# Choosing between GpSimd and VectorE by the port that they share, in a hybrid attention and state-space layer

## The chip, the cores and the metric

The kernel runs on 1 core of one Trainium2 chip. The metric is the device time of one execution in microseconds (us), lower is better. A core has TensorE (PE in the profile, its weight loads PEld), VectorE (DVE), ScalarE (ACT), GpSimd (POOL) and SyncE (SP), which issues the DMAs.

## The reference

One layer over 1024 tokens of width 2048, in float32. The input is projected once, and the columns are split into an attention group and a state-space group.

```python
u = jnp.einsum('bsd,de->bse', h, w_in[layer])
q, k, v, z_attn, q_idx, k_idx, w_idx, z_ssd, xbc, dt_raw = _split_cols(u, IN_WIDTHS)
# rotary positions on a quarter of each head of q, k, q_idx and k_idx
logits = jax.nn.relu(jnp.einsum('bqhd,bsd->bqhs', qib, k_idx32))        # 16 indexer heads
score = jnp.einsum('bqhs,bqh->bqs', logits, wb)                          # then the top 256 keys
...
o_attn = _dsa_attention(q, k, v, q_idx, k_idx, w_idx) * jax.nn.silu(z_attn)
# depthwise conv, chunked scan, gate, grouped RMS norm
o_ssd = _ssd_mixer(xbc, z_ssd, dt_raw, conv_w[layer], conv_b[layer], dt_bias[layer], ...)
mixed = jnp.concatenate([o_attn, o_ssd], axis=-1)
sub = jnp.einsum('bse,ed->bsd', mixed, w_out[layer])
h = _layer_norm(DEEPNORM_ALPHA * h + sub, ln_g[layer], ln_b[layer])
```

## The kernel before, in words

The tokens are worked in two halves of 512 (`h` is 0 or 1). Each float32 operand of a projection is split into a rounded part and a residue, `hi` and `lo`, and three matmuls stand for one product: hi times hi, hi times lo, lo times hi. ScalarE makes `hi` by a copy (`fl.act`); `lo` is `raw - hi`, an operation with two operands in SBUF. The tiles are called `wr` (raw weights), `wh` and `wl` (their two parts), `xh` and `xl` (the input's or the mixed groups' parts), `pj` (projection in PSUM), `a` and `o` (other PSUM tiles, three and one), `u` and `s4` (working tiles in SBUF, of 512 and 1024 columns; the profile writes `s4` as `s`), `cv` (conv input) and `sm` (small columns).

TensorE's stream is the projections (`emit_t`, 128 columns of the weights at a time, two pieces of 1024 columns of `wr` each), later the output projection (`emit_o`). Into it the kernel weaves tasks: rotary positions and indexer scores (`t_misc`, `t_qi`, `t_score`), the selection of keys (`t_topk`), attention (`t_kv`, `t_attn`), the state-space groups (`t_xbc`, `t_ssd`) and the layer norm.

No engine's order is written out by hand. While the program is built, `Flow` keeps a clock for each engine (`Sim`), with a price for each operation, and emits a task's next step when its inputs are done by those clocks and its engines are not too far ahead. So a price or a choice of engine changes the order of all engines after it. On the chip each engine runs its own list in order and waits for semaphores.

`Sim` also models a port to SBUF that VectorE and GpSimd share: `Port.take` moves an operation behind the one that holds the port, and `shares_port` says which operations need it. On GpSimd it is every one with an SBUF operand, on VectorE one with two SBUF operands, or a `tensor_scalar` or copy from SBUF to SBUF. `pick` chooses between the two engines for the residues `wl` and `xl`. All other operations have an engine written into the code: the rotary product with the sine table, one half of the indexer queries' residue, the residues of keys, values and queries, the second of two decay products (`"VG"[k]`), and the sums and gates of the state-space groups go to GpSimd. Every instruction is recorded by one helper, so that the profile gives L290 for all; the tiles tell them apart.

Of the kernel before, what the change touches and what calls it, by code (L numbers as in the profile page):

```python
# [13 lines left out]
ALU = mybir.AluOpType  # L14
# [3 lines left out]
HALF = 512  # L18
P = 128
# [11 lines left out]
N4 = 9  # L31
WAHEAD = 2
KEEP = (0, 0)
WBIAS = 0.0


SKEW = 6
# [63 lines left out]
def in_psum(x):  # L101
    return "PSUM" in str(x.space)
# [10 lines left out]
class Sim:  # L113
# [107 lines left out]
    def shares_port(self, eng, op, outs, ins, n):  # L221
        sb = [x for x in ins if not in_psum(x) and x.free_size() > 1]
        if eng == "G":
            return op != "memset" and len(sb) > 0
        if n < 16 or op in ("max", "match_replace"):
            return False
        if op in ("tensor_scalar", "tensor_copy"):
            return n > 128 and len(sb) == 1 and not in_psum(outs[0])
        return len(sb) >= 2

    def run(self, eng, op, outs, ins, kw):
# [99 lines left out]
class Flow:  # L331
# [92 lines left out]
    def signal(self, e):  # L424
        self.signals.append(e)

    def pick(self, n, bias=0.0):


        if any(e[2] == "V" and e[0] > max(self.t, e[3] + 200) for e in self.sim.port.busy):  # L430
            return "V"
        g = max(self.clk["G"], self.t) + 180 + 2.16 * n
        v = max(self.clk["V"], self.t) + 145 + 1.042 * n
        return "G" if g + bias < v else "V"

    def pump(self, room=2000.0):
        end = self.t + room
# [74 lines left out]
def f32(ap):  # L512
    return ap.bitcast(F)


class Layer:
# [76 lines left out]
    def w_split(self, i):  # L593
        fl = self.fl
        kind, h, t, u = self.stream[i]
        raw = self.wraw.pop(i)
        hi = fl.new("wh" if fl.slots["wh"] else "s4", [P, 1024], R)
        if self.kept(i):
            fl.act(hi, raw)
            fl.free(raw)  # L600
            self.w[i] = hi, self.wlo.pop(i)
            return
        lo = fl.new("wl" if fl.slots["wl"] else "s4", [P, 1024], R)
        cols = [slice(c * 256, (c + 1) * 256) for c in range(4)] if i == 0 else [slice(0, 1024)]
        for c in cols:
            fl.act(hi[:, c], raw[:, c])
            self.sub(fl.pick(c.stop - c.start, WBIAS), lo[:, c], raw[:, c], f32(hi[:, c]))
        cell = fl.last
        fl.free(raw)
        if h == 0 and self.keep(kind, t):  # L610
            fl.add(self.t_keep(kind, t, u, lo, Event(cell)), 1, "keep")
        self.w[i] = (hi, lo)
# [35 lines left out]
    def x_split(self, k):  # L648
        fl = self.fl
        if self.xh[k] is not None:  # L650
            fl.free(self.xh[k], self.xl[k])
            fl.settle(fl.t)
        hi, lo = fl.new("xh", [P, HALF], R), fl.new("xl", [P, HALF], R)
        raw = self.raws.pop(k)
        fl.act(hi, raw)
        self.sub(fl.pick(HALF), lo, raw, f32(hi))
        fl.free(raw)
        self.xh[k], self.xl[k] = hi, lo

# [256 lines left out]
    def rope(self, x, ps, tmp, cos, sin, perm):  # L916

        fl = self.fl
        self.nc.vector.stream_shuffle(tmp, ps, perm)
        yield Need("VG")  # L920
        fl.tt("V", ps, ps, cos, ALU.mult)
        fl.tt("G", tmp, tmp, sin, ALU.mult)
        yield Need("V")
        fl.tt("V", x, ps, tmp, ALU.add)

# [88 lines left out]
    def t_qi(self, h, j, ps):  # L1014
        fl = self.fl
        n = 256 if h == 0 else 512
        s0 = 512 - n
        yield Need("A", u=4, keep=3)
        cos, sin = self.table("ri", h)
        x, tmp = fl.new("u", [P, n]), fl.new("u", [P, n])  # L1020
        a1, a2 = fl.new("u", [P, n], R), fl.new("u", [P, n], R)
        yield Need("V")
        yield from self.rope(x, ps[:, 0:n], tmp, cos[:, s0:], sin[:, s0:], self.SW8)
        fl.free(ps)
        yield Need("A")
        fl.act(a1[0:64], x[0:64])
        fl.act(a2[64:128], x[64:128])
        yield Need("VG")
        self.sub("V", a1[64:128], x[0:64], f32(a1[0:64]))
        self.sub("G", a2[0:64], x[64:128], f32(a2[64:128]))  # L1030
        fl.free(x, tmp)
        blocks = (2, 3) if h == 0 else (4, 5, 6, 7)
        if h not in self.score:
            yield Need("", **({"u": 2} if h == 0 else {"s4": 4}))
            if h not in self.score:
                self.score[h] = {i: fl.new("u" if h == 0 else "s4", [P, 512 if h == 0 else 1024]) for i in blocks}
        if j == 7:
            fl.free(*self.tab["ri", h])
        first = True
        for hh, st in ((0, a1), (1, a2)):  # L1040
            head = 2 * j + hh
            for bi, i in enumerate(blocks):
                q0 = i * P - h * HALF - s0
                lhs = st[:, q0:q0 + P]
                for kh in range(h + 1):
                    m = min((i + 1) * P - kh * HALF, HALF)
                    yield Need("PA", a=1, ev=(self.ev_k[h], self.ev_k[0], self.ev_w[h]))
                    khh, k1, k2 = self.kk[kh]
                    b = fl.new("a", [P, 512])
                    fl.mm(b[:, 0:m], lhs, khh[:, 0:m], stop=False)  # L1050
                    fl.mm(b[:, 0:m], lhs, (k1, k2)[hh][:, 0:m], start=False)
                    fl.add(self.t_score(h, i, kh, m, head, b), 2, f"score{h}", fl.t)
        fl.free(a1, a2)
# [176 lines left out]
    def t_kv(self, h, g, st, total):  # L1230
        fl = self.fl
        w = 512 * (h + 1)
        if g == 1:
            yield Need(ev=(self.ev_att(h, 0),))
        evs = tuple(self.ev_kv[hh, g, x] for hh in range(h + 1) for x in "kv") + tuple(self.ev_q[h, 4 * g + r] for r in range(4)) \
            + tuple(self.ev_z[h, 4 * g + r] for r in range(4)) + (self.ev_mask[4 * h], self.ev_mask[4 * h + 1])
        yield Need(ev=evs, u=4 * (h + 1) + 2, keep=4)
        out = {(x, hh): [fl.new("u", [P, HALF], R) for _ in range(2)] for x in "kv" for hh in range(h + 1)}
        st["kv"] = out
        for (x, hh), (hi, lo) in out.items():  # L1240
            yield Need(u=1)
            raw = fl.new("u", [P, HALF])
            fl.dma(raw, (self.k_sc if x == "k" else self.v_sc)[hh][g])
            yield Need("A")
            fl.act(hi, raw)
            yield Need("G")
            self.sub("G", lo, raw, f32(hi))
            fl.free(raw)
        fl.signal(st["ev"])
        yield Need(ev=(self.ev_att(h, g),))  # L1250
        fl.free(*[t for pair in out.values() for t in pair])
# [5 lines left out]
    def t_attn(self, h, g, st, todo):  # L1257
        fl, nc = self.fl, self.nc
        while todo:
            i, pr = todo.pop(0)  # L1260
            n = (i + 1) * P
# [5 lines left out]
            raw, gate = rg[:, 0], rg[:, 1]  # L1267
            qq = fl.new("u", [P, 2, 2, P], R)
            qh, ql = qq[:, 0], qq[:, 1]
# [8 lines left out]
            yield Need("A")  # L1278
            fl.act(qh, raw)
            yield Need("G")  # L1280
            self.sub("G", ql, raw, f32(qh))
            yield Need("", sm=1)
            sm = fl.new("sm", [P, 16])
            scored = []
            for r in range(2):
                for half in range(-(-n // 512)):
# [3 lines left out]
                    b = fl.new("a", [P, 512])  # L1290
# [4 lines left out]
                    e = Event()  # L1295
# [20 lines left out]
            while kb < nk or ahead:  # L1316
                if kb < nk and len(ahead) < 3:
                    yield Need("P", a=1, u=1, now=True)
                    b = fl.new("a", [P, 256])
# [3 lines left out]
                    e = Event()  # L1323
# [4 lines left out]
                k0, pq, e = ahead.pop(0)  # L1328
# [13 lines left out]
            for r in range(2):  # L1342
                e = 4 * g + heads[r]
# [68 lines left out]
    def t_ssd(self, h, g):  # L1412
        fl, nc = self.fl, self.nc
        sd = getattr(self, f"sd{h}")
        parts = [self.conv[h, g, j] for j in range(4)] + [self.zg[h, g, j] for j in range(2)]
        xs, bt, ct = [parts[0][0], parts[1][0]], parts[2][0], parts[3][0]
        zg = [parts[4][0], parts[5][0]]
# [9 lines left out]
        for cp in range(2):  # L1427
            cs = (2 * cp, 2 * cp + 1)
            yield Need("P", s4=1, u=5, a=1)
            ar = fl.new("s4", [P, 2, 4, P])  # L1430
            bn, xdt, xdd, hs = [fl.new("u", [P, 2, 256]) for _ in range(4)]
            ea = fl.new("u", [P, 2, 2, P])
# [6 lines left out]
            for k, c in enumerate(cs):  # L1439
                if k:  # L1440
                    yield Need("P", a=1)
                b = fl.new("a", [P, 512])
# [10 lines left out]
            b = fl.new("a", [P, 256])  # L1453
# [4 lines left out]
            cbm = bn[:, :, 128:256]  # L1458
# [7 lines left out]
            for k, c in enumerate(cs):  # L1466
# [4 lines left out]
                b = fl.new("a", [P, 256])  # L1471
# [16 lines left out]
            fl.act(ea, ea, AF.Exp)  # L1488
            yield Need("VG")
            for k, c in enumerate(cs):  # L1490
                fl.tt("VG"[k], ar[:, k], ar[:, k], cbm[:, k][:, None, :].to_broadcast([P, 4, P]), ALU.mult)
            k0 = 0 if hcur[0] is not None else 1
            yield Need("P", o=1, a=1)
            b = fl.new("a", [P, 2, 2, P])
# [19 lines left out]
            cl = slice((2 * cp + k0) * P, (2 * cp + 2) * P)  # L1514
            for j in range(2):
                y3 = xs[j][:, cl].rearrange("p (k l) -> p k l", l=P)
                fl.tt("G", y3, y3, ea[:, k0:, j], ALU.add)
            fl.free(bn, xdt, xdd, ea)
            if cp == 0:
                hs0 = hs  # L1520
# [2 lines left out]
        fl.free(hs0, hs)  # L1523
        yield Need("G")
        for j in range(2):
            fl.tt("G", xs[j], xs[j], zg[j], ALU.mult)
        yield Need("A")
        for j in range(2):
            fl.act(zg[j], xs[j], AF.Square)
        yield Need("G")  # L1530
        fl.tt("G", zg[0], zg[0], zg[1], ALU.add)
        yield Need("P", a=1, sm=1)
        sm = fl.new("sm", [P, 4])
        b = fl.new("a", [P, 512])
# [9 lines left out]
        b = fl.new("a", [P, 512])  # L1544
# [7 lines left out]
        for j in range(2):  # L1552
            e = 8 + 2 * g + j
# [159 lines left out]
```

## Time and profile before

| | |
|---|---|
| median of 3 runs | 1815.16 us (1812.81 to 1815.38) |
| profiled execution | 1813.86 us, span 1812.0 us |
| TensorE busy | 1768.7 us, 98% |
| VectorE | 1032.4 us, 57%, 1934 instructions |
| ScalarE | 915.2 us, 51%, 1571 instructions |
| GpSimd | 464.3 us, 26%, 415 instructions |
| mean granted clock of TensorE | 0.994 |

A row of a group gives count, busy time, mean ns of one, and the idle time of its engine before it with what ended it. A row of the timeline gives start, duration, engine, operation, tiles, and in brackets an idle time and its releaser. With TensorE busy 98% of the span, the profile is read by its idle stretches: where they are, and which engine ended them.

### The profile page before, as it was taken

Reading aid. Unit: us, or ns where it says so; the run is one execution under the profiler, and the core shown is the slowest. Engines: PE = TensorE matmul, PEld = TensorE weight load, DVE = VectorE, ACT = ScalarE, POOL = GpSimd, SP = SyncE. Lnnn points to the kernel's source line nnn. Section 1 sums busy time; section 2 is a strip of 40 time slices with the busy share of each in tenths; the row PEclk is TensorE's granted clock in tenths of the full one; section 3 lists DMA queues with packets and bytes.
Section 4 is the critical chain, followed back from the end, with each engine's and each line's share of the span. In section 5 each row is a group of like instructions: output and inputs, shape, how many; then the busy total and the mean of one; then the engine's idle time right before and its main releaser. Section 6 shows DMA issues by size and latency. Waiting matters only on the chain. (4 is left out here: it accounts for less than half of the span.)

```text
span 1812.0 us, 24251 instructions
## 1 busy us (share of the span) xinstructions
PE 1768.7 (98%) x8709; PEld 1474.0 (81%) x8709; DVE 1032.4 (57%) x1934; ACT 915.2 (51%) x1571; POOL 464.3 (26%) x415
## 2 busy tenths in 40 slices
PE   9999999999999999999999999999999999999996
PEld 7878888888888878878887888778888888888885
DVE  7855565555325567766755473465546445547435
ACT  6557673433234555566577768773365333431221
POOL 5310231121213133421212132022322122332123
PEclk9999999999999999999999999999999999999998
DMA  8323334333344542222333333333344344558642
GB/s 275 115 82 105 109 111 126 111 128 120 134 146 131 192 137 76 76 67 70 99 105 109 119 111 122 117 122 140 120 155 156 110 144 131 158 173 278 222 163 93
DMA packets 120424, 238.11 MB, mean 131 GB/s; under 512 B 12784, under 2 KB 50928, under 8 KB 120304
## 3 DMA queue, kind: packets, MB, share of 16 engines
q1 hardware_dynamic: 120304, 236.57, 40.2%
q8 instruction: 68, 1.11, 0.2%
q14 instruction: 52, 0.43, 0.1%
HBM read 204.47 MB, written 32.05 MB: 131 GB/s over the span
## 5 line engine op out<-in xcount | busy, mean ns | idle before, releaser
L290 PE MATMUL pj<-xh,wh 128*128 128x512 f32 (+1 forms) x1696 | 665.0, 392 | 1.8 <-ACT xh L290 1.8
L290 PE MATMUL pj<-xh,wl 128*128 128x512 f32 (+1 forms) x1696 | 650.4, 383 | 0.6 <-DVE wl L290 0.6
L290 PE MATMUL pj<-xl,wh 128*128 128x512 f32 (+1 forms) x1696 | 650.0, 383 | 1.0 <-DVE xl L290 0.5
L290 DVE TENSOR_TENSOR wl<-wr,wh 128x1024 fp32r<-128x1024 f32 (+1 forms) x214 | 270.8, 1265 | 504.9 <-ACT wh L290 478.1
L290 ACT ACTIVATE wh<-wr 128x1024 fp32r<-128x1024 f32 (+1 forms) x272 | 283.8, 1045 | 272.9 <-PE pj L290 218.9
L290 PEld LDWEIGHTS pj<-xh,wl 128*128 128x128 f32 x1696 | 320.3, 189 | 64.8 <-DVE wl L290 1.2
L290 PEld LDWEIGHTS pj<-xh,wh 128*128 128x128 f32 x1696 | 320.7, 189 | 62.0 <-issue 2.9
L290 PEld LDWEIGHTS pj<-xl,wh 128*128 128x128 f32 x1696 | 320.9, 189 | 58.4 <-DVE xl L290 0.9
L290 POOL TENSOR_TENSOR u<-u,u 128x512 f32<-128x512 f32 (+8 forms) x164 | 177.1, 1092 | 509.5 <-DVE u L290 317.5
L290 POOL TENSOR_TENSOR wl<-wr,wh 128x1024 fp32r<-128x1024 f32 (+1 forms) x58 | 139.7, 2408 | 370.6 <-ACT wh L290 359.4
L290 PE MATMUL a<-u,u 128*128 128x512 f32 (+3 forms) x840 | 181.2, 342 | 8.9 <-DVE u L290 5.3
L290 PE MATMUL pj<-wh,xh 128*128 128x512 f32 x464 | 183.1, 395 | 0.7 <-ACT u L290 0.7
L290 PE MATMUL pj<-wl,xh 128*128 128x512 f32 x464 | 180.9, 390 | 0.0
L290 PE MATMUL pj<-wh,xl 128*128 128x512 f32 x464 | 180.8, 390 | 0.0
L290 PEld LDWEIGHTS a<-u,u 128*128 128x128 f32 x840 | 137.4, 189 | 40.9 <-DVE u L290 8.4
L290 ACT ACTIVATE u<-s,sm 128x640 bf16<-128x640 int16 (+7 forms) x132 | 130.1, 985 | 32.4 <-DVE sm L290 29.3
L290 ACT ACTIVATE u<-a 128x256 fp32r<-128x256 f32 (+3 forms) x182 | 61.7, 367 | 153.6 <-PE a L290 98.0
L290 ACT ACTIVATE u<-pj 128x512 f32<-128x512 f32 x90 | 53.4, 594 | 146.8 <-PE pj L290 127.4
L290 ACT ACTIVATE a<-a 128x512 f32<-128x512 f32 (+3 forms) x160 | 75.6, 505 | 80.5 <-PE a L290 76.2
L290 PEld LDWEIGHTS pj<-wh,xl 128*128 128x128 f32 x464 | 87.1, 188 | 18.6
L290 PEld LDWEIGHTS pj<-wh,xh 128*128 128x128 f32 x464 | 87.2, 188 | 17.6 <-ACT u L290 1.2
L290 PEld LDWEIGHTS pj<-wl,xh 128*128 128x128 f32 x464 | 87.3, 188 | 16.3
(120 smaller groups left out, 1758.2 us busy)
## 6 DMA issues: line engine op xcount, KB each, us to landing
wr<-wt SPq DMA_DIRECT2D x211, 512.0 KB, 3.3
wr<-wo SPq DMA_DIRECT2D x61, 512.0 KB, 3.7
s<-arow SPq DMA_DIRECT2D x32, 256.0 KB, 4.6
u<-mx SPq DMA_DIRECT2D x32, 256.0 KB, 4.9
u<-xn SPq DMA_DIRECT2D x32, 256.0 KB, 5.6
out<-u SPq DMA_DIRECT2D x32, 256.0 KB, 2.9
u<-arow SPq DMA_DIRECT2D x64, 64.0 KB, 4.3
mx<-u SPq DMA_DIRECT2D x16, 256.0 KB, 2.4
```

The costliest lines, as they stand in the source:

```text
L290: f(*args, **kw)
```

## The change

Four things. `shares_port` counts VectorE's operations of under 16 columns, and those of exactly 128 columns in the one-operand case. `pick` takes the operands instead of a bias: it starts from the time when they are written, and returns VectorE if VectorE holds the port anywhere between GpSimd's start and end by the model, otherwise whichever engine ends first. A helper `two` calls `pick` and emits the operation there. And the operations that had GpSimd written into the code go through `two`, or through `pick`.

```diff
-        if n < 16 or op in ("max", "match_replace"):
+        if op in ("max", "match_replace"):
             return False
         if op in ("tensor_scalar", "tensor_copy"):
-            return n > 128 and len(sb) == 1 and not in_psum(outs[0])
+            return n >= 128 and len(sb) == 1 and not in_psum(outs[0])
...
-    def pick(self, n, bias=0.0):
-        if any(e[2] == "V" and e[0] > max(self.t, e[3] + 200) for e in self.sim.port.busy):
+    def pick(self, n, *ins):
+        at = self.sim.written(*ins) + Sim.LAT
+        g = max(self.clk["G"], at)
+        end = g + 180 + 2.16 * n
+        if any(e[2] == "V" and e[1] > g and e[0] < end for e in self.sim.port.busy):
             return "V"
-        g = max(self.clk["G"], self.t) + 180 + 2.16 * n
-        v = max(self.clk["V"], self.t) + 145 + 1.042 * n
-        return "G" if g + bias < v else "V"
+        return "G" if end < max(self.clk["V"], at) + 145 + 1.042 * n else "V"
+
+    def two(self, out, a, b, op):
+        self.tt(self.pick(out.free_size(), a, b), out, a, b, op)
...
-            self.sub(fl.pick(c.stop - c.start, WBIAS), lo[:, c], raw[:, c], f32(hi[:, c]))
+            fl.two(lo[:, c], raw[:, c], f32(hi[:, c]), ALU.subtract)
...
-        fl.tt("G", tmp, tmp, sin, ALU.mult)
+        fl.two(tmp, tmp, sin, ALU.mult)
...
-        self.sub("G", a2[0:64], x[64:128], f32(a2[64:128]))
+        fl.two(a2[0:64], x[64:128], f32(a2[64:128]), ALU.subtract)
...
-            self.sub("G", lo, raw, f32(hi))
+            fl.two(lo, raw, f32(hi), ALU.subtract)
...
-                fl.tt("VG"[k], ar[:, k], ar[:, k], cbm[:, k][:, None, :].to_broadcast([P, 4, P]), ALU.mult)
+                fl.tt(fl.pick(512, ar, bn), ar[:, k], ar[:, k], cbm[:, k][:, None, :].to_broadcast([P, 4, P]), ALU.mult)
...
-                fl.tt("G", y3, y3, ea[:, k0:, j], ALU.add)
+                fl.two(y3, y3, ea[:, k0:, j], ALU.add)
...
-            fl.tt("G", xs[j], xs[j], zg[j], ALU.mult)
+            fl.two(xs[j], xs[j], zg[j], ALU.mult)
```

The query residue of `t_attn`, `x_split` and the sum of the squared gates change in the same way. In the two programs GpSimd's list shrinks from 420 instructions to 220, and VectorE's grows from 1898 to 2098; TensorE has 8406 and SyncE 777 in both.

Two places of the program, in the order of the built kernels. The first is GpSimd's list in the first indexer heads, around 50 to 75 us of the profile before; `u_62` is the sine table, `wl` a weight residue of 1024 columns. Before:

```order
L290 MEMSET u_110_726 64x512
L290 TENSOR_TENSOR u_127_809<-u_124_806,u_127_809 64x256
L290 TENSOR_TENSOR u_135_891<-u_135_891,u_62_396 128x256
L290 TENSOR_TENSOR wl_147_949<-wr_140_901,wh_146_948 128x1024
L290 TENSOR_TENSOR u_137_893<-u_134_890,u_137_893 64x256
L290 TENSOR_TENSOR u_152_993<-u_152_993,u_62_396 128x256
L290 TENSOR_TENSOR wl_162_1043<-wr_148_962,wh_161_1042 128x1024
```

VectorE's list of the changed kernel at the same weight residue, with the indexer scores (`u_101` gathers them from the PSUM tiles `a`):

```order
L289 STREAM_SHUFFLE u_139_908<-pj_130_826 128x256
L289 TENSOR_TENSOR pj_130_826<-pj_130_826,u_61_395 128x256
L289 TENSOR_TENSOR u_139_908<-u_139_908,u_62_396 128x256
L289 TENSOR_TENSOR u_138_907<-pj_130_826,u_139_908 128x256
L289 TENSOR_TENSOR wl_143_916<-wr_131_833,wh_142_915 128x1024
L289 TENSOR_SCALAR u_101_678<-a_132_854,wsc0_187 128x384
L289 SCALAR_TENSOR_TENSOR u_101_678<-a_133_857,wsc0_187,u_101_678 128x384
L289 TENSOR_TENSOR wl_147_949<-wr_137_886,wh_146_948 128x1024
L289 TENSOR_TENSOR u_140_909<-u_138_907,u_140_909 64x256
```

The residue `wl_147`, the sine products and the half of the query residue now stand in VectorE's list, between the reads that free the PSUM tiles.

The second place is the rotary position of a query head of the second half, around 1138 us of the profile before, on VectorE. Before, the product with the sine table stands in GpSimd's list, and VectorE goes on with the states (`cdec`) meanwhile:

```order
L290 STREAM_SHUFFLE u_1540_9798<-pj_1532_9706 32x512
L290 TENSOR_TENSOR pj_1532_9706<-pj_1532_9706,u_1526_9686 32x512
L290 TENSOR_TENSOR u_1519_9624<-u_1511_9593,cdec1_196 128x256
L290 TENSOR_TENSOR u_1519_9624<-u_1519_9624,a_1541_9800 128x256
L290 TENSOR_TENSOR u_1539_9797<-pj_1532_9706,u_1540_9798 32x512
```

After:

```order
L289 STREAM_SHUFFLE u_1542_9827<-pj_1534_9753 32x512
L289 TENSOR_TENSOR pj_1534_9753<-pj_1534_9753,u_1527_9726 32x512
L289 TENSOR_TENSOR u_1542_9827<-u_1542_9827,u_1528_9727 32x512
L289 TENSOR_TENSOR u_1541_9826<-pj_1534_9753,u_1542_9827 32x512
```

The whole rotary position is one run on VectorE, and nothing stands between its product and its sum.

More of the change, by code (lines that the diff above doesn't have):

```diff
@@ L33 @@
 KEEP = (0, 0)
-WBIAS = 0.0
 SKEW = 6
@@ L655, in x_split @@
         fl.act(hi, raw)
-        self.sub(fl.pick(HALF), lo, raw, f32(hi))
+        fl.two(lo, raw, f32(hi), ALU.subtract)
         fl.free(raw)
@@ L1246, in t_kv @@
             yield Need("G")
-            self.sub("G", lo, raw, f32(hi))
+            fl.two(lo, raw, f32(hi), ALU.subtract)
             fl.free(raw)
@@ L1280, in t_attn @@
             yield Need("G")
-            self.sub("G", ql, raw, f32(qh))
+            fl.two(ql, raw, f32(qh), ALU.subtract)
             yield Need("", sm=1)
@@ L1530, in t_ssd @@
         yield Need("G")
-        fl.tt("G", zg[0], zg[0], zg[1], ALU.add)
+        fl.two(zg[0], zg[0], zg[1], ALU.add)
         yield Need("P", a=1, sm=1)
```

## The prediction

> **What bounds the kernel now.** I read the busy times first, then windows, then the list of what TensorE waited for, then the timeline around its longest waits. Everything below is summed against the profiled execution (span 1812.0 us, time 1813.86 us); the median of the runs is 1815.16 us, 1.3 us more, and that is added at the end. About 0.2% (3.6 us) is what a measurement of this kernel can tell from no change.
>
> ```profile
> PE 1768.7 (98%) x8709; PEld 1474.0 (81%) x8709; DVE 1032.4 (57%) x1934; ACT 915.2 (51%) x1571; POOL 464.3 (26%) x415
> ```
>
> TensorE is the bound: 1768.7 of 1812.0 us, so 43.3 us are idle. The change leaves the number of its instructions as it is (8406 in the program before and after), and only idle time can be won. Windows say where it lies (columns: length, then busy PE, PEld, DVE, ACT, POOL, the granted clock, DMA share, GB/s):
>
> ```profile
> 0.00:50.00 50.00, 45.52 (x286) 39.49 (x287) 37.89 (x57) 30.58 (x59) 26.71 (x37) 0.97 0.78 259
> 50.00:100.00 50.00, 47.18 (x277) 40.69 (x277) 42.99 (x67) 29.64 (x54) 16.13 (x16) 0.97 0.31 105
> 650.00:700.00 50.00, 48.01 (x231) 39.33 (x229) 40.48 (x76) 29.24 (x57) 22.33 (x20) 1.00 0.30 92
> 1750.00:1800.00 50.00, 45.49 (x201) 37.36 (x199) 23.51 (x39) 4.92 (x6) 15.85 (x12) 1.00 0.27 92
> 1800.00:1812.00 12.00, 0.00 (x0) 0.00 (x0) 7.55 (x10) 2.22 (x3) 3.79 (x3) 0.53 0.38 131
> ```
>
> The first 50 us hold 4.5 us of idle time and the end 4.5 + 12.0 = 16.5 us. The last 835 rows of TensorE's program are the same in both, and so are the last rows of the other engines, where the layer norm ends, so the end stays. That leaves 43.3 - 4.5 - 16.5 = 22.3 us of short waits in between. The list of waits (total us, times, longest) names them:
>
> ```profile
> PE a L290 <- DVE u L290: 5.5, 7, 1.9
> PE a L290 <- POOL sm L290: 4.3, 2, 2.4
> PE a L290 <- ACT u L290: 4.0, 1, 4.0
> ...
> PE a L290 <- DVE s L290: 1.8, 4, 0.6
> ...
> PE a L290 <- DVE ddt L290: 1.2, 1, 1.2
> PE o L290 <- DVE sm L290: 1.2, 2, 0.8
> ...
> PE a L290 <- POOL u L290: 0.8, 1, 0.8
> ```
>
> The longest wait for VectorE, at 64.48 us, in the timeline:
>
> ```profile
> 63.38 2.38 POOL L290 TENSOR_TENSOR wl<-wr,wh 128x1024 fp32r<-128x1024 f32 x1 [1.65 <-ACT wh L290]
> 63.57 2.27 DVE L290 SCALAR_TENSOR_TENSOR sm<-dt,nea 128x64 f32<-128x64 f32 x1
> 65.77 0.60 DVE L290 TENSOR_SCALAR u<-a,wsc 128x384 f32<-128x384 f32 x1
> 66.43 1.96 PE L290 MATMUL a<-u,u 128*128 128x512 f32 x4 [1.95 <-DVE u L290]
> ```
>
> GpSimd subtracts a weight tile with two SBUF operands. VectorE's 64-column operation, which also has two, starts behind it and ends when GpSimd does, 2.27 us later; the evacuation that frees TensorE's buffer comes after it. The same at 1064 us, where a product of 512 columns takes 1.67 us instead of 0.69 (row `u<-u,u 128x512` below):
>
> ```profile
> 1061.88 2.38 POOL L290 TENSOR_TENSOR wl<-wr,wh 128x1024 fp32r<-128x1024 f32 x1 [3.59 <-ACT wh L290]
> ...
> 1063.13 1.67 DVE L290 TENSOR_TENSOR s<-s,u 128x512 f32<-128x512 f32 x1
> ...
> 1064.95 1.09 PE L290 MATMUL o<-s,u 128*64 128x128 f32 x16 [0.80 <-DVE sm L290]
> ```
>
> The wait at 64 us costs more than itself, as two windows show:
>
> ```profile
> 63.22:66.64 3.42, 1.47 (x12) 1.27 (x11) 3.23 (x5) 0.80 (x3) 3.10 (x2) 1.00 0.51 162
> 66.64:70.05 3.41, 3.41 (x13) 2.82 (x13) 2.53 (x6) 1.67 (x3) 0.00 (x0) 0.50 0.48 154
> ```
>
> After 3.42 us in which TensorE was busy for 1.47, the next 3.41 us run at half the clock and lose 1.7 us of work. The Trainium skill (TensorE: Matmul & The Clock Gate, section "Why this matters for your kernels") asks only that idle gaps stay under about 3 us; by that this gap of 1.95 us would have kept the clock and my sum would be 1.7 us less. The trace has the half clock behind it, so I go by the row.
>
> **The change part by part.** By the two programs, 200 operations move from GpSimd to VectorE: 51 weight residues of 1024 columns, 40 of 128x512, 51 of 128x256, 20 rope products of 32x512, and 38 smaller ones. Their prices on the two engines (mean ns behind the comma):
>
> ```profile
> L290 POOL TENSOR_TENSOR wl<-wr,wh 128x1024 fp32r<-128x1024 f32 x56 | 138.2, 2468 | 366.6 <-ACT wh L290 355.5 <-DVE s L290 11.1
> L290 POOL TENSOR_TENSOR u<-u,u 128x512 f32<-128x512 f32 x42 | 55.6, 1332 | 71.4 <-DVE u L290 43.2 <-ACT u L290 23.8 <-PE pj L290 4.1
> L290 POOL TENSOR_TENSOR u<-u,u 32x512 f32<-32x512 f32 x20 | 25.6, 1280 | 172.9 <-DVE u L290 172.9
> L290 POOL TENSOR_TENSOR u<-u,u 128x256 f32<-128x256 f32 x32 | 23.6, 756 | 74.6 <-DVE u L290 72.1 <-DMA u<-ri 2.4
> ```
>
> ```profile
> L290 DVE TENSOR_TENSOR wl<-wr,wh 128x1024 fp32r<-128x1024 f32 x212 | 269.9, 1273 | 498.8 <-ACT wh L290 472.1 <-PE pj L290 7.0 <-DMA u<-arow 5.7
> L290 DVE SCALAR_TENSOR_TENSOR s<-a,wsc,s 128x512 f32<-128x512 f32 x75 | 54.7, 747 | 17.7 <-ACT a L290 16.8
> L290 DVE SCALAR_TENSOR_TENSOR u<-u,mv,u 128x512 f32<-128x512 f32 x48 | 48.0, 1020 | 6.6 <-DMA u<-h 5.7
> L290 DVE TENSOR_TENSOR u<-u,cdec 128x256 f32<-128x256 f32 x24 | 16.2, 674 | 0.1
> L290 DVE TENSOR_TENSOR u<-pj,u 32x512 f32<-32x512 f32 x20 | 13.5, 676 | 7.6 <-POOL u L290 7.4
> L290 DVE TENSOR_TENSOR u<-u,a 128x256 f32<-128x256 f32 x24 | 10.1, 421 | 6.1 <-PE a L290 4.0
> L290 DVE TENSOR_TENSOR u<-u,u 128x512 f32<-128x512 f32 x6 | 4.0, 686 | 0.1
> ```
>
> GpSimd loses 51 x 2.47 + 40 x 1.33 + 51 x 0.76 + 20 x 1.28 = 244 us, and some 38 x 1.0 = 38 us for the rest: 464 becomes about 180. VectorE gains 51 x 1.27 + 40 x 0.69 + 51 x 0.42 + 20 x 0.68 = 127 us, and 38 x 0.6 = 23: about 150. Against that, VectorE's two-operand operations no longer sit through GpSimd's. How much that returns is bounded below by two groups: 48 x (1.020 - 0.747) + 24 x (0.674 - 0.421) = 19 us, the reference of each being the like operation with one operand in PSUM; above it by the 244 us that leave GpSimd. I take 70 us, nearer the low end, because GpSimd was busy only 26% of the time. VectorE then stands at 1032 + 150 - 70 = 1112 us, 61%. All this lies beside TensorE; on the path lie only the waits:
>
> - *Waits that go.* From the list I count as the port's: 1.95 at 64 us and 0.6 more of the 5.5 for `DVE u`; 1.3 of the 1.8 for `DVE s`; 1.0 of 1.2 for `DVE ddt`; 0.8 of 1.2 for `o <- DVE sm` (the 1064 place); 0.6 of the 0.8 for `POOL u`, since a product of 512 columns comes 1.33 - 0.69 us sooner on VectorE; 0.6 of the 4.3 for `POOL sm`; 0.7 of the 4.0 for `ACT u` (next fence); and 0.6 of smaller ones. That is 8.15, and 1.7 us of clock: 9.85 us. The bounds are 3.65 (64 us alone) and 22.3 + 1.7.
>
> ```profile
> 1138.99 1.29 POOL L290 TENSOR_TENSOR u<-u,u 32x512 f32<-32x512 f32 x1 [12.30 <-DVE u L290]
> ...
> 1139.42 1.14 DVE L290 TENSOR_TENSOR u<-u,cdec 128x256 f32<-128x256 f32 x1
> ...
> 1142.11 0.83 ACT L290 ACTIVATE u<-s,sm 128x640 bf16<-128x640 f32 x1 [4.17 <-DVE sm L290]
> ...
> 1144.11 1.28 ACT L290 ACT_TABLE_LOAD   x1
> ...
> 1147.52 0.66 PE L290 MATMUL a<-c,u 128*128 128x128 f32 x4 [4.05 <-ACT u L290]
> ```
>
> Here the rope product on GpSimd stretches VectorE's 0.42 us to 1.14, ScalarE waits for a later VectorE operation, and the copy that TensorE wants is queued behind. Only the stretch goes; the rest of this wait is order.
>
> - *Waits that come.* What is queued behind a moved operation on VectorE starts up to 1.27 us later, and TensorE waits for some of it. Nothing shows these waits yet. Bounds: 0 (they fall where TensorE has other rows to run) and 5.65 us (as much comes as I took from the rows that wait for VectorE). I take 1.5, nearer 0, because VectorE's load grows by 8% only.
> - *The start.* Two weight pieces of 256 columns move in front of the first input residues: at most 2 x 0.42, at least 0; I take 0.2, since the second piece alone stands in the way.
> - *Port counting for operations under 16 columns, and 128 columns.* It changes only the model: order, no work. Cost 0, kept in the rivals. No DMA is added: SyncE's queue holds the same 777, a few of them in another place.
>
> Sum: 1813.9 - 9.85 + 1.5 + 0.2 = 1805.7, and 1.3 for the median: **1807 us**.
>
> **The rivals.** *VectorE's queue becomes the bound (slower).* VectorE was busy 42.99 of 50 us from 50 to 100 and 40.48 from 650 to 700. If a weight residue of 1.27 us stands before an evacuation that TensorE wants, TensorE waits it out. This loses from about 11 of the 51 on, (9.85 + 3.6) / 1.27; with 20 it gives 1807 - 1.5 + 25 = 1830, with 14 about 1823. For it: these two windows. Against it: the 212 residues there already cost TensorE few waits, and GpSimd's turn held VectorE up as long anyway (2.27 us above). The Trainium skill (Perfetto Trace Analysis, "Optimizing Scalar/DVE Operations") says that offloading a saturated VectorE, even to GpSimd, may make sense, and adds that the shared port may spoil it; the rows at 63 us agree with the second half.
>
> *The waits only move (same).* TensorE's order is redrawn from its row 335 on, and ScalarE's table loads grow from 47 to 57. At 1144 us such a load of 1.28 us lies in the chain of the longest wait. If three or four of the ten extra ones do, or one new wait brings a half-clock window (1.7 us), 4 to 6 us come back: 1811 to 1814.
>
> *The model fits better everywhere (faster still).* If half of the other 12 us of middle waits goes too, 1801. For it: small operations wait for GpSimd in the trace (2.27 us above) and the model had them free. Against it: the waits for `POOL sm` and `ACT u` are order, not port.
>
> **How the numbers follow.** Forecast 0.42, moved waits 0.27, better model 0.15, VectorE's queue 0.16. Forecast and better model are faster by over 0.2% (below 1811.5), less a little of the forecast's upper edge and with a little of the moved waits': 0.56. Same 0.27, slower 0.17. The range runs from 1799 (better model, with a little to spare) to 1818 (half of the port's waits return, 4.9, new ones cost 5.65 instead of 1.5, and the runs of one kernel lie 2.6 us apart): the two ends leave out mostly the slower rival.
>
> **What would show it.** Right: POOL near 180 us, DVE near 1110; no two-operand operation on VectorE above twice its clean time after 60 us; no wait of 2 us at 64 us and full clock there; TensorE busy still 1769 and idle in the middle about 13 us. Wrong: waits for `DVE wl` or `DVE u` above 10 us in sum (the queue), or waits for ACT behind table loads (moved waits).

## The result and the profile after

The changed kernel takes 1799.3 us (median of 4 runs, 1798.58 to 1799.71) against 1814.7 us for the kernel before on the same chip: a ratio of 0.9916 with an interval of 0.9899 to 0.9933, 15.4 us less. The forecast was 1807 us with 1799 to 1818: the side is right, the mechanism in part, and the gain is nearly twice the 8 us that the sum gave.

Busy times of the changed kernel:

```profile
span 1797.9 us, 24116 instructions
...
PE 1767.6 (98%) x8709; PEld 1473.3 (82%) x8709; DVE 1077.6 (60%) x2134; ACT 926.6 (52%) x1581; POOL 162.7 (9%) x215
```

TensorE does the same work, 1767.6 us, and is idle for 30.3 us instead of 43.3. GpSimd lost 301.6 us, and VectorE gained only 45.2, although the moved operations are 150 us of work by the prediction's prices: by that estimate about 105 us of sitting through GpSimd's turns are gone. Windows of the changed kernel (length, busy PE, PEld, DVE, ACT, POOL, granted clock, DMA share, GB/s):

```profile
0.00:50.00 50.00, 45.16 (x275) 39.44 (x276) 37.15 (x63) 29.80 (x58) 18.47 (x28) 0.93 0.76 258
50.00:100.00 50.00, 48.27 (x290) 41.02 (x288) 43.52 (x84) 31.79 (x57) 0.93 (x2) 1.00 0.33 107
900.00:1250.00 350.00, 347.68 (x1714) 287.82 (x1713) 203.61 (x424) 250.66 (x407) 21.61 (x25) 1.00 0.38 120
1750.00:1797.90 47.90, 31.39 (x139) 25.67 (x137) 26.48 (x42) 6.09 (x8) 17.24 (x14) 0.86 0.25 88
```

The start holds 4.8 us of idle time and the end 47.90 - 31.39 = 16.5, as before, so the middle has 30.3 - 4.8 - 16.5 = 9.0 us where it had 22.3. Most of it went from 900 to 1250 us, where the second half's keys are selected: 2.3 us idle instead of 10.2, by the same window of the kernel before and its three longest waits for ScalarE and GpSimd, 8.4 us in sum:

```profile
900.00:1250.00 350.00, 339.82 (x1672) 281.33 (x1671) 193.67 (x377) 253.43 (x413) 86.62 (x70) 1.00 0.36 115
...
964.93 1.16 PE L290 MATMUL a<-c,sm 128*128 128x128 f32 x8 [2.40 <-POOL sm L290]
...
1147.52 0.66 PE L290 MATMUL a<-c,u 128*128 128x128 f32 x4 [4.05 <-ACT u L290]
...
1208.13 1.16 PE L290 MATMUL a<-c,sm 128*128 128x128 f32 x8 [1.93 <-POOL sm L290]
```

From 50 to 100 us VectorE is busy for 43.52 us, hardly more than the 42.99 before, and GpSimd for 0.93 instead of 16.13: by these sums GpSimd's work there cost VectorE about as much in waiting as it costs VectorE to do it. What TensorE waits for now (total us, times, longest):

```profile
PE a L289 <- DVE u L289: 2.2, 5, 1.1
PE a L289 <- DVE ddt L289: 2.1, 2, 1.7
PE pj L289 <- ACT xh L289: 1.9, 2, 1.0
PE pj L289 <- POOL xl L289: 1.4, 2, 1.1
...
PE a L289 <- DVE s L289: 1.1, 5, 0.4
...
PE a L289 <- POOL sm L289: 0.3, 1, 0.3
```

The 4.0 us for `ACT u` is gone, and 4.3 us for `POOL sm` are 0.3. At the place of the 64 us wait, the timeline shows the 64-column operation that took 2.27 us, and a third of the wait. What is left of it stands behind a weight residue (`wl`) in VectorE's own queue:

```profile
60.95 0.23 DVE L289 SCALAR_TENSOR_TENSOR sm<-dt,nea 128x64 f32<-128x64 f32 x1
...
63.92 1.22 DVE L289 TENSOR_TENSOR wl<-wr,wh 128x1024 fp32r<-128x1024 f32 x1
65.06 0.61 DVE L289 TENSOR_SCALAR u<-a,wsc 128x384 f32<-128x384 f32 x1
...
65.72 1.38 PE L289 MATMUL a<-u,u 128*128 128x512 f32 x4 [0.61 <-DVE u L289]
```

The operation takes 2.27 us beside GpSimd's 2.38 us subtraction, and 0.23 alone. The Trainium skill (SBUF — State Buffer, "Summary: rules for kernel authors") says that when VectorE's operation has two SBUF inputs and GpSimd's reads SBUF, the second to issue blocks fully until the first finishes. The rows at 63.38 and 63.57 us of the kernel before agree: VectorE's operation ends 0.08 us after GpSimd's.

### The profile page after: what moved, and what is told of

Its sections match the earlier page's. It is cut to its first block, busy times and chain, and to the rows that moved or that the text cites. A ratio compares the mean times of both kernels' runs of the same rounds, so it can differ in the third digit from the quotient of the medians.

```text
span 1797.9 us, 24116 instructions
## 1 busy us (share of the span) xinstructions
PE 1767.6 (98%) x8709; PEld 1473.3 (82%) x8709; DVE 1077.6 (60%) x2134; ACT 926.6 (52%) x1581; POOL 162.7 (9%) x215
## 4 chain that ended last, share of the span: by engine, by line
PE 84%; DVE 7%; ACT 6%; issue 2%; DMA 1%; SPq 0%; POOL 0%; DVEq 0%; ACTq 0%
PE pj L289 71%; PE a L289 10%; PE o L289 4%; DVE u L289 3%; ACT u L289 3%; DVE wl L289 2%; ACT wh L289 1%; DVE s L289 1%; DMA wr<-wt 1%; DVE pj L289 1%; ACT L289 1%; ACT a L289 0%; ACT s L289 0%; ACT pj L289 0%; ACT cv L289 0%
## 5 line engine op out<-in xcount | busy, mean ns | idle before, releaser
L289 DVE TENSOR_TENSOR wl<-wr,wh 128x1024 fp32r<-128x1024 f32 (+1 forms) x264 | 322.1, 1221 | 457.0 <-ACT wh L289 446.5
L289 DVE TENSOR_TENSOR u<-u,u 64x512 fp32r<-64x512 f32 (+7 forms) x161 | 89.4, 569 | 10.5 <-ACT u L289 9.2
L289 DVE TENSOR_TENSOR u<-a,u 128x256 fp32r<-128x256 f32 (+2 forms) x160 | 64.9, 437 | 35.6 <-ACT u L289 32.4
```

Source lines behind the costliest of these rows:

```text
L289: f(*args, **kw)
```

## The experiments

The runs are set against three theories. Theory "port": VectorE no longer waits for GpSimd's turns, and that is the gain. Theory "order" (later "foresight"): the kernel's order now fits what the engines do, and that is the gain. Theory "luck": any other order would do. In the runs that change the model or a constant alone, a "draw" is the order that the planner makes with one set of constants. Each ratio is taken against the kernel before as it was timed on the same chip beside that run.

| run | median us | ratio to the kernel before (interval) |
|---|---|---|
| order_kept_on_V | 1828.4 | 1.0070 (1.0055 to 1.0085) |
| new_order_on_G | 1828.4 | 1.0071 (1.0053 to 1.0089) |
| model_alone | 1804.0 | 0.9937 (0.9921 to 0.9954) |
| change_old_model | 1803.6 | 0.9933 (0.9918 to 0.9948) |
| before_lat80 | 1805.9 | 0.9948 (0.9930 to 0.9967) |
| before_slack25 | 1818.8 | 1.0023 (1.0013 to 1.0034) |
| after_lat80 | 1797.7 | 0.9903 (0.9882 to 0.9924) |
| after_slack27 | 1796.0 | 0.9895 (0.9877 to 0.9913) |
| pick_no_port | 1800.6 | 0.9924 (0.9903 to 0.9944) |
| all_on_V | 1795.6 | 0.9895 (0.9875 to 0.9914) |
| model_alone_slack25 | 1806.9 | 0.9954 (0.9938 to 0.9971) |
| start_on_V | 1795.4 | 0.9894 (0.9876 to 0.9912) |

**Engines without the order, and the order without the engines.** In the first, the emission model of the kernel before is told GpSimd, and the instruction is issued on VectorE; TensorE's list does not differ by a row.

```diff
+        if eng == "g":
+            e = Engine(self, self.nc.vector.engine, "G")   # booked as GpSimd, issued on VectorE
...
-        fl.tt("G", tmp, tmp, sin, ALU.mult)
+        fl.tt("g", tmp, tmp, sin, ALU.mult)      # and so at the other places of the change
```

> The orders of TensorE, ScalarE and SyncE are exactly those of the kernel before, as if GpSimd still did its part; but all that the change lets choose (about 240 operations with two SBUF operands) is issued on VectorE at its place in the emission. Theory 'port' (the gain is VectorE's freedom from GpSimd's turns): most of the gain is there without any new order, 1800 to 1806 us, idle of TensorE in the middle 10 to 15 us. Theory 'order' (the gain is that the steps stand in a better order): no gain, 1811 to 1818 us, since the order is the old one. Theory 'luck' (any new order loses the 4 us wait at 1143 us): that wait is still there, 1811 to 1816.

1828.4 us, 13 us slower than before: outside what all three theories said. VectorE does lose its waits for GpSimd (busy 1092.5 us with 242 more operations; the changed kernel moves 200, this run all that it lets choose), but TensorE waits more: its waits for `DVE u` are 13.2 us instead of 5.5, and it is idle for 50.2 us instead of 43.3. Its busy time grows too, by 8.2 us; the windows at half the clock add up to 17.1 us ahead of the end instead of 10.2, which by an estimate is 3.4 of them, and the rest stays open. One of the waits, on VectorE and TensorE, with the window behind it:

```profile
PE a L290 <- DVE u L290: 13.2, 15, 2.5
...
238.92 1.23 DVE L290 TENSOR_TENSOR wl<-wr,wh 128x1024 fp32r<-128x1024 f32 x1 [3.00 <-ACT wh L290]
240.06 0.68 DVE L290 TENSOR_TENSOR u<-u,u 128x512 f32<-128x512 f32 x1
...
240.80 1.44 PE L290 MATMUL a<-o,u 128*128 128x1 f32 x6 [2.47 <-DVE u L290]
...
240.39:247.21 6.82, 6.41 (x19) 5.44 (x20) 1.49 (x7) 0.28 (x1) 1.17 (x2) 0.50 0.23 77
```

and the same product on GpSimd in the kernel before:

```profile
238.74 1.27 POOL L290 TENSOR_TENSOR u<-u,u 128x512 f32<-128x512 f32 x1 [3.06 <-ACT u L290]
...
240.06 1.05 PE L290 MATMUL a<-o,u 128*128 128x1 f32 x8 [0.83 <-POOL u L290]
```

The sum of the squared gates is half as long on VectorE, but it stands there behind a weight residue that waits for ScalarE, while GpSimd, in the kernel before, stood idle for 3.06 us until its input came. The counterpart issues on GpSimd what the changed kernel moved, but for the weight and input residues:

```diff
-        self.tt(self.pick(out.free_size(), a, b), out, a, b, op)
+        e = self.pick(out.free_size(), a, b)
+        self.tt("v" if e == "V" else e, out, a, b, op)   # booked as VectorE, issued on GpSimd
```

> The orders of TensorE, ScalarE and SyncE are exactly those of the changed kernel, as if VectorE did the moved operations; but the some 140 that had GpSimd written into the code are issued on GpSimd again (the weight residues stay where the change puts them). Theory 'port': VectorE sits through GpSimd's turns again, two thirds of the gain lost, 1807 to 1815 us. Theory 'order': nearly all of the gain stays, 1799 to 1804.

1828.4 us as well: TensorE is idle for 48.2 us, 17.9 more than in the changed kernel, and busy for 14.4 more, with 34.1 us at half the clock ahead of the end instead of 6.8. GpSimd's list now has places that were made for VectorE:

```profile
PE a L289 <- POOL u L289: 11.4, 6, 4.8
PE o L289 <- POOL s L289: 3.1, 2, 2.3
```

"Order" in its plain form falls with this run, "port" in its plain form with the first. In these runs an order is worth its gain only on the engines that it was made for: the wrong engines cost the old order 13 us and the new one 29.

**The two halves of the change by themselves.** The model's rule alone, and the choice of engines alone:

```diff
-        if n < 16 or op in ("max", "match_replace"):      # model_alone has these two new lines and no
+        if op in ("max", "match_replace"):                # other; change_old_model all but these two
...
-            return n > 128 and len(sb) == 1 and not in_psum(outs[0])
+            return n >= 128 and len(sb) == 1 and not in_psum(outs[0])
```

> The kernel before, with the new rule for which operations need the port in the emission model alone (under 16 columns, and 128 columns, counted); every operation stays on its engine, but for the residues that the old choice moves. Theory 'order': the model foresees more of the waits, so 1805 to 1810. Theory 'port': the waits are still there, 1812 to 1818.

> The changed kernel with the old rule for which operations need the port in the emission model (under 16 and 128 columns not counted); the choice between the engines is the new one. Theory 'port': the same as the changed kernel, 1797 to 1803. Theory 'order': a good part of the gain is lost, 1804 to 1812.

1804.0 and 1803.6 us: the model's half gives 11.5 us, the choice's half 11.9, and both together 15.4, so the two gains mostly overlap. Either half by itself already removes most of the waits for `ACT u` and `POOL sm` (8.3 us before, 0.6 and 0.9 us left). In the run of the model alone GpSimd's work is all there, and VectorE is stretched as before (`u<-u,cdec` 629 ns, 674 before):

```profile
PE 1765.9 (98%) x8709; PEld 1471.7 (82%) x8709; DVE 1035.2 (57%) x1929; ACT 914.5 (51%) x1571; POOL 478.2 (27%) x420
...
L290 DVE TENSOR_TENSOR u<-u,cdec 128x256 f32<-128x256 f32 x24 | 15.1, 629 | 0.1
...
900.00:1250.00 350.00, 348.01 (x1717) 288.72 (x1716) 206.91 (x383) 257.87 (x421) 96.37 (x71) 1.00 0.37 119
```

The window says where its gain lies: 2.0 us idle from 900 to 1250 us, 8.2 less than before. There VectorE's operations of four columns steer the selection of keys, and they are what the new rule counts. Their rows in the kernel before, in the run of the model alone, and in the changed kernel:

```profile
L290 DVE SCALAR_TENSOR_TENSOR sm<-sm 128x4 f32<-128x4 f32 x32 | 8.8, 276 | 1.1
L290 DVE TENSOR_TENSOR sm<-sm 128x4 f32<-128x4 f32 x32 | 8.4, 262 | 12.4 <-ACT u L290 12.4
```

```profile
L290 DVE SCALAR_TENSOR_TENSOR sm<-sm 128x4 f32<-128x4 f32 x32 | 11.0, 343 | 1.1
L290 DVE TENSOR_TENSOR sm<-sm 128x4 f32<-128x4 f32 x32 | 7.7, 241 | 22.1 <-ACT u L290 22.1
```

```profile
L289 DVE SCALAR_TENSOR_TENSOR sm<-sm 128x4 f32<-128x4 f32 x32 | 5.2, 164 | 1.1
L289 DVE TENSOR_TENSOR sm<-sm 128x4 f32<-128x4 f32 x32 | 5.0, 156 | 11.4 <-ACT u L289 11.2
```

In the kernel before they take 7 us more than in the changed one, and the old model had them free. With the model alone they are no shorter (18.7 us in sum, 17.2 before), so that half's gain is not that VectorE is spared. My reading is that, with the waits foreseen, the matmuls that depend on them are placed behind work that is ready; the runs show the place and the size of the gain, not this step by itself. The rule has a second part, operations of exactly 128 columns, and no run separates the two.

**Is it luck?** Two constants that have nothing to do with the port redraw the order of either kernel: `LAT`, 70 to 80 ns, and `SLACK`, 2600 to 2500 or 2700 ns.

> The kernel before with one constant of the emission model moved that has nothing to do with the port: the delay between engines is 80 ns instead of 70. TensorE's order is redrawn in 1466 lines. Theory 'luck' (the order before was an unlucky draw, and most others are 10 us faster): 1800 to 1808 us. Theory 'foresight' (the port that the model had wrong costs the 10 us in any draw): 1811 to 1820.

> The same with another constant: engines may run 2500 instead of 2600 ns ahead of TensorE, 674 lines of TensorE's order differ. 'Luck': 1800 to 1808 us. 'Foresight': 1811 to 1820.

> The changed kernel with the delay of 80 ns, 712 lines of TensorE's order differ. 'Foresight': 1796 to 1802 us as the changed kernel, whatever the draw. 'Luck': anything from 1797 to 1812, and the changed kernel lies at the low end of it.

> The changed kernel with engines up to 2700 ns ahead, 1395 lines of TensorE's order differ. 'Foresight': 1796 to 1802 us. 'Luck': 1797 to 1812.

The kernel before gives 1805.9, 1814.7 and 1818.8 us; the changed kernel 1797.7, 1799.3 and 1796.0. So the sign is no luck: the three draws with the change all lie below the three without, and their means are 15.5 us apart. The size in one draw is in part luck: the draws of the kernel before span 13 us, more than one half of the change gives, and 1805.9 lies where "luck" had put it, outside the 1811 to 1820 of "foresight". With `LAT` at 80 in both kernels the change is worth 8.2 us and not 15.4: that redraw alone already removes the wait of 4.0 us for `ACT u`, and 2.4 of the 4.3 us for `POOL sm` are left. A longer `LAT` also makes the model more cautious, which may be why that draw is the best one; this was not told apart. So the model's rule got a second draw, against the 1818.8 of the old rule:

> The kernel before with the new rule of the emission model alone, in another draw (2500 ns ahead, where the kernel before took 1818.8). If the model's rule by itself is worth the 11 us that its first draw showed: 1804 to 1809 us. If that was luck: 1812 to 1820.

1806.9, 11.9 us less than with the old rule. Two draws, 11.5 and 11.9 us, speak for the rule itself. But the old rule's best draw, 1805.9, lies between the rule's own 1804.0 and 1806.9, and the rule was not run with `LAT` at 80, so what it is worth over many draws stays open.

**Does the question about the port pay, or the free choice?** The two lines that return VectorE when it holds the port are taken out of `pick`:

```diff
-        if any(e[2] == "V" and e[1] > g and e[0] < end for e in self.sim.port.busy):
-            return "V"
```

> The changed kernel without the question about the port in the choice: an operation goes to whichever of the two engines would end it first by its clock alone (the emission model still lets the port block). GpSimd then keeps 151 operations with two operands, 33 weight residues among them, instead of 81 and 8. Theory 'port' (the rule is what pays): VectorE is stretched again, half of the gain lost, 1804 to 1811 us. Theory 'free choice' (what pays is that GpSimd's own slow operations leave the chains that TensorE waits for, and the port is second): 1797 to 1803.

1800.6 us, which is what "free choice" said, with 280.5 us of work left on GpSimd. TensorE's waits for GpSimd are 7.0 us in this run, as in the kernel before, against 3.1 in the changed kernel. Its first 50 us show the full clock where the changed kernel's show 0.93, which may be luck of that draw. The draws with the question are 1 to 5 us faster, with intervals that overlap, so what the question is worth by itself stays open within that.

**Is VectorE's queue a danger?** The other end, everything on VectorE with an order made for it, and the input residues of the start in addition (in the draw with 2700 ns):

```diff
-        self.tt(self.pick(out.free_size(), a, b), out, a, b, op)
+        self.tt("V", out, a, b, op)                        # all_on_V
...
-            split(k, h1, "VVG"[k % 3])
+            split(k, h1, "V")                              # start_on_V, with SLACK 2700
...
-                        split(m - 4, h0, "VG"[m % 2])
+                        split(m - 4, h0, "V")
```

> The changed kernel, but everything that may choose goes to VectorE: GpSimd keeps 39 operations with two operands (the start, the powers and the end). My rival of VectorE's queue: with 42 more operations VectorE is late where it is full, 1803 to 1815 us. Theory 'port' or 'free choice': GpSimd's last 42 are worth little either way, 1796 to 1802.

> The draw of 1796.0 us (2700 ns ahead), with the input residues of the first 36 us all on VectorE too, 12 of which the changed kernel leaves on GpSimd by its code; TensorE's order is the same. In the changed kernel TensorE waits there for a residue on GpSimd and has half the clock behind it. Theory 'port': the last stretched operations go, 1 to 3 us faster, 1793 to 1795. VectorE's queue: the start is full (37.9 of 50 us before), so 1797 to 1802.

1795.6 and 1795.4 us. With an order made for it, VectorE at 1099.6 us holds up little (TensorE waits for it by 5.9 us in all, 7.5 in the changed kernel), and the rule of the change is no better here than leaving GpSimd only what the code fixes on it. `start_on_V` is the fastest kernel of the study, 19.7 us below the kernel before, but its 0.6 us against its own draw of 1796.0 are within the intervals. The row of `all_on_V`:

```profile
PE 1765.9 (98%) x8709; PEld 1473.3 (82%) x8709; DVE 1099.6 (61%) x2176; ACT 925.7 (52%) x1579; POOL 108.2 (6%) x173
```

## Why the prediction was right, and where its size failed

- *What bounds, what is untouched.* TensorE's work (1767.6 us) and the end (16.5 us) stayed. Right.
- *The engines.* GpSimd 162.7 us (forecast 180), VectorE 1077.6 (1112). By the prediction's prices the stretch that goes is 105 us, not the 70 that I took near the low end of its bounds. The sign "no two-operand operation above twice its clean time" did not hold throughout: at 1306.66 us a product of two columns takes 1.06 us beside a GpSimd subtraction, where the mean of its 48 is 0.22.
- *The 64 us wait and its half clock.* From 1.95 to 0.61 us, where the sum took all of it off, and the windows behind it are at full clock. Right.
- *The waits for VectorE.* They were 12.5 us; the sum took 5.65 off and put 1.5 on, which leaves 8.35. The list of the changed kernel has 7.5. Right.
- *Port counting in the model, "order, no work, cost 0".* This is the term that was mis-sized. Alone it gave 11.5 and 11.9 us in two draws. I kept it as a rival (the model fits better everywhere, 1801 us) at 0.15; with 1799.3 us that rival is what came, on top of the forecast. What I gave for it does not carry it: the operation of 2.27 us has 64 columns and two SBUF operands, and the old rule, which left out those under 16, already counted it. The four-column rows above are what the model had free.
- *"The rest of this wait is order".* I left 3.7 of the 4.3 us for `POOL sm` and 3.3 of the 4.0 for `ACT u` standing because they were order and not port. All but 0.3 us of the two went, 8.0 us where the sum had 1.3, and these 6.7 us are nearly the whole of what the gain has over the forecast's 8. They went because order changed. The step that failed is to treat order as fixed in a kernel whose order is computed from the prices that change. But a redraw without the change (`LAT` at 80) removes the `ACT u` wait too, and there the change is worth 8.2 us: that the size came out at nearly twice the forecast is in part the luck of the draw.
- *The clock behind the wait at 1144 us.* It was not priced. Half the clock followed there as well, 1.7 us by the reckoning used at 64 us; the changed kernel shows the full clock in every 50 us from 50 to 1750.

```profile
1145.25:1148.66 3.41, 1.14 (x7) 1.06 (x8) 0.00 (x0) 3.40 (x7) 1.27 (x1) 1.00 0.17 67
1148.66:1152.08 3.42, 3.42 (x9) 2.66 (x9) 2.15 (x5) 2.39 (x4) 0.00 (x0) 0.50 0.38 97
```

- *Idle time in the middle, "about 13 us".* By the sum's own terms it is 22.3 - 8.15 + 1.5 = 15.7, since the 1.7 us of clock are not idle time; 9.0 were measured. "The other 12 us" of the rival has the same slip, and is 14.2.
- *`DVE ddt`.* I took 1.0 of its 1.2 us off. It rose to 2.1, 1.7 of them at one place. From VectorE's copy `ac` to its subtraction `ddt` 2.1 us pass there in both kernels (667.91 to 670.05 us before, 662.14 to 664.29 after), with a table load of ScalarE of 1.28 us in between, so this chain did not get shorter when GpSimd's work left.
- *New waits on VectorE, 1.5 us.* They are not told apart from the old ones: VectorE's rows in the list are 7.5 us in all, and 5.9 in `all_on_V`. The rival of VectorE's queue fell in its form, but `order_kept_on_V` shows that its mechanism is real where nobody plans for it: 13 us.
- *The start, 0.2 us.* Idle time there rose from 4.5 to 4.8 us; but half the clock held for 6.8 us (12.57 to 19.40) instead of 3.4, which costs 1.7 us more and was not forecast. Not every draw has it: `start_on_V` and `pick_no_port` show the full clock over their first 50 us.

## What to carry to other kernels

Where a planner makes the order, a wrong price costs twice: the operation is late, and everything placed by it stands in the wrong spot. So do not put an edit of the planner's rules at nothing because it is "no work": here the rule alone gave 11.5 and 11.9 us in two draws. Move an operation to another engine together with the order, since a like move without it lost 13 us here; and before a gain of under 1% is put down to a cause, redraw the order of both kernels once or twice with a constant that has nothing to do with it; the same change was worth 15.4 us in one draw and 8.2 in another.

## What the runs showed of the hardware

A 64-column operation with two SBUF operands on VectorE takes 0.23 us alone and took 2.27 beside GpSimd's 2.38 us subtraction, ten times as long. The clock fell to half after a window of 3.42 us in which TensorE was busy for 1.47 us in the kernel before, and in the changed kernel's start after 4.33 us busy of 6.83:

```profile
5.74:12.57 6.83, 4.33 (x25) 3.34 (x25) 3.95 (x9) 5.21 (x14) 2.55 (x3) 1.00 1.05 370
12.57:19.40 6.83, 6.21 (x29) 6.21 (x30) 5.65 (x8) 4.60 (x8) 2.31 (x3) 0.50 0.82 274
```

No single wait of TensorE that falls in the first of these is longer than 1.15 us; half the clock followed all the same, as it did behind the 1.95 us at 64 us in the kernel before. The busy share of one window does not settle it by itself: in the kernel before, 1.68 us busy of 3.42 were followed by the full clock, and in the changed kernel's start 1.94 of 3.41 by half.

```profile
960.84:964.26 3.42, 1.68 (x10) 1.28 (x8) 1.79 (x4) 1.60 (x4) 0.41 (x1) 1.00 0.22 91
964.26:967.67 3.41, 2.74 (x16) 2.45 (x17) 3.41 (x14) 2.70 (x6) 0.76 (x2) 1.00 0.49 156
```

```profile
9.16:12.57 3.41, 1.94 (x12) 1.34 (x10) 2.00 (x4) 2.82 (x8) 1.02 (x2) 1.00 1.09 384
```
